# Loading a 2048-element scale vector with one DMA and one broadcast in place of four DMAs and two broadcasts

## The chip, the cores and the metric

The kernel runs on one core of a Trainium2 chip. The metric is device time in microseconds (us) of one execution. The engines that matter here are ScalarE (ACT), VectorE (DVE), GpSimd (POOL), SyncE (SP, which here only issues DMAs), and the 16 DMA engines of the core, which carry every byte between the chip's main memory and the on-chip memory of 128 partitions. A DMA that SP or ACT issues goes into a queue of its issuer (in the profile, q1 is SP's and q10 is ACT's), and is carried out as packets on the DMA engines. TensorE is not used.

## The reference

```python
def setup_inputs():
    B, S, D = 8, 512, 2048
    return {"x": randn(B, S, D) as float32, "gamma": randn(D) as float32}

def reference(x, gamma):
    x_rep = np.repeat(x, 2, axis=1)
    rms = np.sqrt((x_rep ** 2).mean(axis=-1, keepdims=True) + 1e-6)
    return (x_rep / rms * gamma[None, None, :]).astype(np.float32)
```

Each of the 4096 rows of x is divided by its root mean square, multiplied by gamma, and written twice. The input is 33.6 MB, the output 67.1 MB, and gamma 8 KB.

## The kernel before, in words

The 4096 rows are cut into four blocks of 1024 rows. A block is loaded by one DMA of 8.4 MB (`load`, line 50) in which each partition gets 8 whole rows, 65,536 contiguous bytes. Its output, 16.8 MB, leaves by two DMAs of 8.4 MB (`store`, line 53), each again 65,536 contiguous bytes per partition. So there are 4 loads and 8 stores, twelve large DMAs of the same size, all on SP's queue and in the order in which `four` issues them.

There is one large buffer `y` with three regions of 8 rows per partition: `first`, `second` and `third`. `four(n, m, ...)` handles two blocks. It loads block n across the end of `first` and the start of `second`, calls `constants`, loads block m into `third`, and then works through four half blocks. For each half block ACT squares and sums four rows (`squares`, lines 63 and 67), DVE takes the reciprocal (line 76) and multiplies each row by it and by gamma (line 77, `scalar_tensor_tensor`, from the region that holds the input to the region that holds the output), and the result row is copied next to itself by ACT or DVE (`repeat`, line 84). Then SP issues the store. The kernel calls `four` twice, for blocks 0 and 1 and for blocks 3 and 2. The second pair of loads has to wait until the stores that still read their regions have landed.

The order on every engine is as written (`manual_schedule`, line 86); no scheduler moves anything. The first load is issued by SP, then `constants` (lines 122 to 141) puts its work on DVE, ACT and POOL, and then SP issues the second load.

`constants` brings gamma to all 128 partitions. Its DMAs are issued by ACT. One brings the first 2000 elements as 16 pieces of 125 elements (500 bytes), laid down in partition 0 with a step of 256 elements, in a part of `y` that no load touches so early (line 127). Three more bring the last 48 elements, 16 each (64 bytes; line 133). POOL then copies partition 0 to all partitions into `gamma_b`: the 2000 elements (line 137) when the first DMA has landed, and the last 48 (line 141) when the other three have landed. The first multiply on DVE waits for both. It overwrites the place where the pieces of gamma lay, so it also has to come behind POOL's reading of them.

Of the kernel before, what the change touches and what calls it, by code (L numbers as in the profile page):

```python
# [1 line left out]

# [4 lines left out]


@with_exitstack
def kernel(  # L10
    ctx: ExitStack,
    tc: tile.TileContext,
    x: bass.AP,
    gamma: bass.AP,
    out: bass.AP,
):
    nc = tc.nc
    P = nc.NUM_PARTITIONS
    f32 = mybir.dt.float32
    Act = mybir.ActivationFunctionType  # L20
    Alu = mybir.AluOpType

    B, S, D = x.shape
    Bo, So, Do = out.shape
    R = So // S
    assert R == 2 and D == Do and B == Bo and So == S * R
    eps = 1e-6
    inv_d = 1.0 / float(D)


    K = 4
    N = B * S
    ntiles = N // (P * K)
    assert N % (P * K) == 0 and ntiles == 8
    H = 2
    x_t = x.rearrange("b s d -> (b s) d").rearrange("(n p k) d -> n p k d", p=P, k=H * K)
    out_t = out.rearrange("b s d -> (b s) d").rearrange("(n p h j) d -> n h p (j d)", p=P, h=H, j=K * R)

    singles = ctx.enter_context(tc.tile_pool(name="singles", bufs=1))
    rows = ctx.enter_context(tc.tile_pool(name="rows", bufs=1))  # L40
    junk = ctx.enter_context(tc.tile_pool(name="junk", bufs=1, space=bass.MemoryType.PSUM))
    small = ctx.enter_context(tc.tile_pool(name="small", bufs=4))

    y = rows.tile([P, 3 * K * R, D], f32, name="y")
    first, second, third = 0, K * R, 2 * K * R

    def load(n, at):
        nc.sync.dma_start(out=y[:, at : at + H * K, :], in_=x_t[n])  # L50

    def store(n, h, to):
        nc.sync.dma_start(
            out=out_t[n, h], in_=y[:, to : to + K * R, :].rearrange("p j d -> p (j d)")
        )

    def squares(at, rows):

        n = len(rows)
        ss = small.tile([P, n], f32, name=f"ss{n}")  # L60
        for c, k in enumerate(rows):
            sq = junk.tile([P, D], f32, name="sq")
            nc.scalar.activation(  # L63
                out=sq[:], in_=y[:, at + k, :], func=Act.Square, accum_out=ss[:, c : c + 1]
            )
        rms = small.tile([P, n], f32, name=f"rms{n}")
        nc.scalar.activation(out=rms[:], in_=ss[:], func=Act.Sqrt, scale=inv_d, bias=eps_t[:])  # L67
        return rms

    def scale(at, to, rows, rms, at_once=K):  # L70
        n = len(rows)
        rstd = small.tile([P, n], f32, name=f"rstd{n}")
        for c, k in enumerate(rows):
            if c % at_once == 0:
                part = slice(c, min(c + at_once, n))
                nc.vector.reciprocal(out=rstd[:, part], in_=rms[:, part])  # L76
            nc.vector.scalar_tensor_tensor(  # L77
                out=y[:, to + R * k, :], in0=y[:, at + k, :], scalar=rstd[:, c : c + 1],
                in1=gamma_b[:], op0=Alu.mult, op1=Alu.mult,
            )  # L80

    def repeat(to, k0, k1, copy):
        y_r = y[:, to + R * k0 : to + R * k1, :].rearrange("p (k r) d -> p k r d", r=R)
        copy(out=y_r[:, :, 1, :], in_=y_r[:, :, 0, :])  # L84

    ctx.enter_context(tc.manual_schedule())

    half = K // 2
    up, down = list(range(K)), list(range(K - 1, -1, -1))

    def four(n, m, constants, at_once):


        load(n, first + K)
        constants()
        load(m, third)
        for rows, n_at_once in ((up[:half], half), (up[half:], at_once)):
            scale(first + K, first, rows, squares(first + K, rows), n_at_once)
        repeat(first, 0, half, nc.scalar.copy)
        repeat(first, half, K, nc.vector.tensor_copy)  # L100
        store(n, 0, first)
        scale(second, second, down, squares(second, down))
        repeat(second, half, K, nc.scalar.copy)
        repeat(second, 0, half, nc.vector.tensor_copy)
        store(n, 1, second)
        roots = [squares(third + h * K, up) for h in range(H)]
        scale(third, first, up, roots[0])
        repeat(first, 0, half, nc.scalar.copy)
        repeat(first, half, K, nc.scalar.copy)
        store(m, 0, first)  # L110
        scale(third + K, third, up, roots[1])
        repeat(third, 0, K, nc.scalar.copy)
        store(m, 1, third)

    gamma_b = singles.tile([P, D], f32, name="gamma_b")
    G, E = 16, 3
    C = D // G - E
    gamma_s = y[0:1, 0:2, :].rearrange("p k (c d) -> p (k c) d", c=G // 2)
    gamma_t = y[0:1, 2, :]
    eps_t = singles.tile([P, 1], f32, name="eps_t")  # L120

    def constants():
        nc.vector.memset(eps_t, eps)  # L123

        root = singles.tile([P, 1], f32, name="root")[:]
        nc.scalar.activation(out=root, in_=eps_t[:], func=Act.Sqrt)  # L126
        nc.scalar.dma_start(
            out=gamma_s[0:1, :, :C],
            in_=gamma[: G * C].rearrange("(p c d) -> p c d", p=1, c=G),
        )  # L130
        for c in range(E):
            at = G * C + c * G
            nc.scalar.dma_start(
                out=gamma_t[0:1, c * G : (c + 1) * G],
                in_=gamma[at : at + G].partition_broadcast(1),
            )
        nc.gpsimd.partition_broadcast(  # L137
            out_ap=gamma_b[:, : G * C].rearrange("p (c d) -> p c d", c=G),
            in_ap=gamma_s[0:1, :, :C],
        )  # L140
        nc.gpsimd.partition_broadcast(out_ap=gamma_b[:, G * C :], in_ap=gamma_t[0:1, : E * G])  # L141

    four(0, 1, constants, 1)
    four(3, 2, lambda: None, half)


# [1 line left out]
_INS = ['x', 'gamma']  # L148
_OUTS = [((8, 1024, 2048), 'float32')]


# [23 lines left out]
```

## Time and profile before

| what | value |
|---|---|
| median of 3 runs | 238.1 us (238.01 to 238.22) |
| the profiled execution | 237.99 us, its span 236.2 us |
| DMA traffic | 100.68 MB, mean 426 GB/s over the span |
| ACT busy | 110.2 us (47%) |
| DVE busy | 84.5 us (36%) |
| POOL busy | 2.8 us (1%) |
| first load issued | 0.72 us |
| first square on ACT starts | 22.68 us |
| first multiply on DVE starts | 27.34 us |
| first store issued | 39.27 us |

The span is what the profile shows of the execution, from its first to its last instruction; 1.8 us of the execution's time lie around it. A row of the profile that names a line and an engine, such as "L77 DVE", stands for all instructions of that source line on that engine, with their number, the total of their busy time, the mean of one, and the idle time of the engine ahead of them with what ended it. The trace also records every DMA packet with its queue, start, duration and size, and the prediction makes use of these records.

### The profile page before, as it was taken

The numbers are of one execution on the slowest core, as the hardware profiler recorded it, in microseconds if no ns is written. First come the engines' busy times: TensorE is split into PE (matmuls) and PEld (weight loads), VectorE is DVE, ScalarE is ACT, GpSimd is POOL, SyncE is SP. The second block draws the span as 40 slices with busy tenths as digits, with TensorE's granted clock in tenths as the row PEclk, the third lists the DMA queues.
The fourth block names the chain that finished last, engine by engine and source line by source line (L and its number), as shares of the span: only waits on it lengthen the run. The fifth ranks groups of instructions, "written<-read, shape, count | busy, mean of one in ns | idle before, by whom it ended". The sixth has DMA issues, their size and how long they took to land.

```text
span 236.2 us, 226 instructions
## 1 busy us (share of the span) xinstructions
DVE 84.5 (36%) x48; ACT 110.2 (47%) x86; POOL 2.8 (1%) x6
## 2 busy tenths in 40 slices
DVE  0000396594699500000000007928919992000000
ACT  2001989479998470000000049991999957400000
POOL 0210000000000000000000000000000000000000
DMA  9898989989898989989898998989898998989894
GB/s 355 357 533 355 533 355 477 411 377 511 355 533 357 522 366 466 422 377 511 355 533 355 488 400 377 511 355 533 355 533 355 477 411 377 511 355 533 355 533 178
DMA packets 1767, 100.68 MB, mean 426 GB/s; under 512 B 230, under 2 KB 230, under 8 KB 230
## 3 DMA queue, kind: packets, MB, share of 16 engines
q1 hardware_dynamic: 1728, 100.66, 98.8%
q10 hardware_dynamic: 38, 0.01, 0.0%
q14 instruction: 1, 0.01, 0.0%
HBM read 33.56 MB, written 67.11 MB: 426 GB/s over the span
## 4 chain that ended last, share of the span: by engine, by line
DMA 45%; ACT 26%; DVE 12%; issue 2%; DVEq 0%
DMA y<-in_x_dram 26%; DMA out_dram<-y 20%; ACT sq L63 15%; DVE y L77 12%; ACT y L84 11%; ACT rms L67 1%; DVE rstd L76 0%; DVEq L77 0%
## 5 line engine op out<-in xcount | busy, mean ns | idle before, releaser
L63 ACT ACTIVATE sq<-y 128x2048 f32<-128x2048 f32 x32 | 60.1, 1878 | 73.0 <-DMA y<-in_x_dram 72.3
L77 DVE SCALAR_TENSOR_TENSOR y<-y,rstd,gamma_b 128x2048 f32<-128x2048 f32 x32 | 73.8, 2349 | 1.5 <-DMA out_dram<-y 0.9
L84 ACT COPY y<-y 128x4096 f32<-128x4096 f32 (+1 forms) x10 | 42.6, 4283 | 18.9 <-DVE y L77 18.2
L76 DVE RECIPROCAL rstd<-rms 128x4 f32<-128x4 f32 (+2 forms) x11 | 1.9, 168 | 109.2 <-ACT rms L67 109.2
L84 DVE COPY y<-y 128x4096 f32<-128x4096 f32 x4 | 9.2, 2294 | 0.1
L63 ACT ACTIVATION_READ_ACCUMULATOR sq<-y 128x1 f32 x32 | 6.0, 186 | 0.0
L67 ACT ACTIVATE rms<-ss,eps_t 128x4 f32<-128x4 f32 (+1 forms) x10 | 3.0, 296 | 0.3
L137 POOL PARTITION_BROADCAST gamma_b<-y x1 | 2.2, 2243 | 10.2 <-DMA y<-in_gamma_dram 10.2
L126 ACT ACT_TABLE_LOAD x1 | 1.3, 1283 | 0.7 <-PEq L159 0.7
L141 POOL PARTITION_BROADCAST gamma_b<-y x1 | 0.3, 323 | 10.2 <-DMA y<-in_gamma_dram 10.2
L123 DVE MEMSET eps_t<- 128x1 f32 x1 | 0.1, 59 | 0.8 <-PEq L159 0.8
L126 ACT ACTIVATE root<-eps_t 128x1 f32<-128x1 f32 x1 | 0.2, 202 | 0.0
L159 POOL MEMSET const-bfloat16-1.0<- 128x1 bf16 x1 | 0.1, 101 | 0.0
L159 POOL MEMSET const-uint8-127<- 128x1 uint8 x1 | 0.1, 101 | 0.0
L159 POOL MEMSET const-float32-0.0<- 128x1 f32 x1 | 0.1, 98 | 0.2 <-issue 0.2
L159 POOL MEMSET const-float32-1.0<- 128x1 f32 x1 | 0.1, 98 | 0.0
## 6 DMA issues: line engine op xcount, KB each, us to landing
out_dram<-y SPq DMA_DIRECT2D x8, 24.9
y<-in_x_dram SPq DMA_DIRECT2D x4, 31.4
y<-in_gamma_dram ACTq DMA_DIRECT2D x3, 0.1 KB
y<-in_gamma_dram ACTq DMA_DIRECT2D x1, 7.8 KB, 9.6
```

The costliest lines, as they stand in the source:

```text
L63: nc.scalar.activation(out=sq[:], in_=y[:, at + k, :], func=Act.Square, accum_out=ss[:, c : c + 1])
L67: nc.scalar.activation(out=rms[:], in_=ss[:], func=Act.Sqrt, scale=inv_d, bias=eps_t[:])
L76: nc.vector.reciprocal(out=rstd[:, part], in_=rms[:, part])
L77: nc.vector.scalar_tensor_tensor(out=y[:, to + R * k, :], in0=y[:, at + k, :], scalar=rstd[:, c : c + 1], in1=gamma_b[:], op0=Alu.mult, op ...
L84: copy(out=y_r[:, :, 1, :], in_=y_r[:, :, 0, :])
L123: nc.vector.memset(eps_t, eps)
L126: nc.scalar.activation(out=root, in_=eps_t[:], func=Act.Sqrt)
L137: nc.gpsimd.partition_broadcast(out_ap=gamma_b[:, : G * C].rearrange("p (c d) -> p c d", c=G), in_ap=gamma_s[0:1, :, :C],)
L141: nc.gpsimd.partition_broadcast(out_ap=gamma_b[:, G * C :], in_ap=gamma_t[0:1, : E * G])
L159: nc = _bacc.Bacc("TRN2", target_bir_lowering=False, num_devices=1)
```

## The change

The four DMAs of `constants` become one, and the two broadcasts become one. The staging place for gamma is now one row of partition 0 (2048 elements, contiguous), written as 16 pieces of 128 elements that lie one behind the other on both sides. Nothing else is touched: the loads, the stores, the arithmetic and their order stay.

```diff
     gamma_b = singles.tile([P, D], f32, name="gamma_b")
-    G, E = 16, 3
-    C = D // G - E
-    gamma_s = y[0:1, 0:2, :].rearrange("p k (c d) -> p (k c) d", c=G // 2)
-    gamma_t = y[0:1, 2, :]
+    G = 16
+    gamma_s = y[0:1, 0, :].rearrange("p (c d) -> p c d", c=G)
     eps_t = singles.tile([P, 1], f32, name="eps_t")
...
         nc.scalar.dma_start(
-            out=gamma_s[0:1, :, :C],
-            in_=gamma[: G * C].rearrange("(p c d) -> p c d", p=1, c=G),
+            out=gamma_s, in_=gamma.rearrange("(p c d) -> p c d", p=1, c=G)
         )
-        for c in range(E):
-            at = G * C + c * G
-            nc.scalar.dma_start(
-                out=gamma_t[0:1, c * G : (c + 1) * G],
-                in_=gamma[at : at + G].partition_broadcast(1),
-            )
         nc.gpsimd.partition_broadcast(
-            out_ap=gamma_b[:, : G * C].rearrange("p (c d) -> p c d", c=G),
-            in_ap=gamma_s[0:1, :, :C],
+            out_ap=gamma_b[:].rearrange("p (c d) -> p c d", c=G), in_ap=gamma_s
         )
-        nc.gpsimd.partition_broadcast(out_ap=gamma_b[:, G * C :], in_ap=gamma_t[0:1, : E * G])
```

## The prediction

> **What bounds the kernel now.** I read the page's busy shares first. No compute engine is above 47%, so none of them is the bound by itself. The DMA rows say what is: 100.66 MB of the 100.68 MB are on SP's queue, and the DMA engines are busy for 98.8% of the span.
>
> ```profile
> span 236.2 us, 226 instructions
> DVE 84.5 (36%) x48; ACT 110.2 (47%) x86; POOL 2.8 (1%) x6
> DMA packets 1767, 100.68 MB, mean 426 GB/s; under 512 B 230, under 2 KB 230, under 8 KB 230
> q1 hardware_dynamic: 1728, 100.66, 98.8%
> q10 hardware_dynamic: 38, 0.01, 0.0%
> ```
>
> The view of stretches shows where the missing 1.2% lies: in the first 39 us and behind 234 us, not in the middle (last two columns: DMA share, GB/s; a packet counts where it starts, hence 1.01).
>
> ```profile
> 2.00:41.00 39.00, 11.93 (x8) 17.60 (x17) 2.57 (x2) 1.00 0.94 407
> 41.00:118.00 77.00, 30.33 (x16) 36.94 (x27) 0.00 (x0) 1.00 1.01 435
> 118.00:157.00 39.00, 11.85 (x7) 17.43 (x16) 0.00 (x0) 1.00 0.99 430
> 157.00:234.00 77.00, 30.34 (x16) 36.90 (x27) 0.00 (x0) 1.00 1.01 436
> ```
>
> The packet records make it exact. The twelve large DMAs are 1536 packets of 65,536 B, 96 on each of 16 engines. One takes 2.418 us, the next starts 0.004 us before its end, so 96 take 96 x 2.414 = 231.7 us. The first packets start at 1.73 to 2.06 us and take 2.86 to 3.27 us (0.45 to 0.85 more than later ones), engines lose up to 0.67 us more where reading starts again at 118 us, and the last packets end between 234.5 and 235.0 us. Following each engine from packet to packet I find no other idle time on any engine. The time is thus: start, 96 packets on the last engine, and 1.2 us behind them.
>
> The page's chain of waits has ACT and DVE on it, but this chain follows one path of releases. What counts is whether a store is ever issued too late. The DMA issues and the landings in the packet records give two tight places: the first stores of the two passes are issued at 39.27 and 155.20 us, and the first engine runs out of loads at 40.93 and 157.21. The later stores of each pass have 3.4 us or more.
>
> Gamma's own path, from the view of instructions in order:
>
> ```profile
> 0.72 0.86 SPq L50 DMA_DIRECT2D y<-in_x_dram  x2
> 0.89 0.60 ACTq L127 DMA_DIRECT2D y<-in_gamma_dram  x1
> 1.53 0.67 ACTq L133 DMA_DIRECT2D y<-in_gamma_dram  x1
> 2.23 0.50 ACTq L133 DMA_DIRECT2D y<-in_gamma_dram  x2
> 10.62 2.24 POOL L137 PARTITION_BROADCAST gamma_b<-y  x1 [10.19 <-DMA y<-in_gamma_dram]
> 22.68 1.88 ACT L63 ACTIVATE sq<-y 128x2048 f32<-128x2048 f32 x1 [20.47 <-DMA y<-in_x_dram]
> 23.02 0.32 POOL L141 PARTITION_BROADCAST gamma_b<-y  x1 [10.16 <-DMA y<-in_gamma_dram]
> 27.07 0.17 DVE L76 RECIPROCAL rstd<-rms 128x2 f32<-128x2 f32 x1 [26.23 <-ACT rms L67]
> 27.34 4.61 DVE L77 SCALAR_TENSOR_TENSOR y<-y,rstd,gamma_b 128x2048 f32<-128x2048 f32 x2
> 39.27 16.96 SPq L53 DMA_DIRECT2D out_dram<-y  x2
> ```
>
> The reader is to see that gamma_b is ready at 23.34 us, that DVE starts its first multiply at 27.34, and that it was waiting for ACT's square root, not for POOL. Gamma is 4.0 us early.
>
> **The change part by part.**
>
> *ACT's issues.* Four issues (0.60, 0.67, 0.21 and 0.26 us) become one. ACT has nothing to do before 22.68 us, when the first load has landed, so this is worth 0. The cover is 20 us.
>
> *Broadcasts.* 2.24 + 0.32 us become one of 2048 elements; by the larger row 2.24 x 2048/2000 = 2.30 us, by both 2.57. It starts when the new DMA lands. The earliest old landing let POOL start at 10.62 us, the latest at 23.02, so gamma_b is ready between 12.9 and 25.6 us. Both are before 27.07, when DVE has its root: 0. If the new DMA landed with the slowest old row, 1.5 us of cover would still be left.
>
> *Waits.* DVE's second multiply, ACT's first copy and SP's first store each lose their wait for the three small DMAs. These landed by 23 us and the waiters ran later (29.6, 32.03, 39.27): 0.
>
> *DMA packets.* Here is the only thing that touches the bound. In the records the old main DMA is 16 packets of 500 B, one per engine, 26 ns each. Around it the next large packet starts 20 ns behind the end of the former instead of 4 ns before: 24 ns per engine, and 6 ns more for the packet that signals the end. The three small DMAs are not spread out. Each is one packet of 64 B, all on one engine (call it A), and each costs A another 6 to 8 ns twice; on A the large packet behind the 500 B also takes 93 ns longer. A falls 0.14 us behind the other engines; with the common 0.03 it pays 0.17 us.
>
> What the new DMA is, I take from the built program: since its 16 pieces lie one behind the other on both sides, it stands there as one run of 1x2048, of the same form as the three 1x16; the old main DMA stands as 1x16x125. The 1x16 form moved as one packet on one engine, so I expect one packet of 8,192 B on A and nothing on the other 15. The Trainium skill, DMA: Bandwidth & Descriptors, Why a DMA increments its semaphore by 16 and not by 1, says that the engines are chosen by the slowest dimension that is not 1, and that software can split a contiguous 2048-element load so that 16 engines share it. This trace has the unsplit case (64 B on one engine) and no split one. The Trainium skill, same title, Rules for kernel authors, speaks against the change: an outermost dimension under 16 confines a DMA to as many engines. By it the sum is the one that follows; split, it would be that of the first rival.
>
> The nearest row for 8,192 B is one packet that fetches instructions amid the stores:
>
> ```profile
> q14 instruction: 1, 0.01, 4.8%
> ```
>
> It was recorded with 0.309 us at 75.06 us, and the engine that carried it (call it B) fell 0.246 us behind. So A pays 0.25 to 0.31 us plus 0.006 for the signal, in place of 0.17: +0.08 to +0.15 us on A. The other 15 engines save 0.03 each.
>
> *The sum at the end.* B ends last (0.50 us behind the first), A 0.13 us before B. After: B 0.03 earlier, A 0.05 before B to 0.05 behind it. The end moves by -0.03 to +0.02 us if B stays where it is. Whether the instruction fetch still falls on B at 75 us is open, as ACT has fewer instructions; without it B ends 0.25 us earlier and the next engine, 0.13 us before, sets the end; behind 118 us it would be as much later. That is -0.13 to +0.15 us.
>
> *The first store.* The first load lands when its slowest engine signals, at 22.116 us, and this is A. With A 0.08 to 0.15 us later, ACT's squares, the multiplies, the copies and the store's issue all move by as much: 39.35 to 39.43 us. From issue to first packet the first load took 1.00 us, and 1.34 to the last engine. So the store's packets are there at 40.3 to 40.8 us, and engines get free from 40.90: covered, with 0.1 to 0.6 us left. The same holds at 155 us with more room.
>
> Sum against the profiled execution (237.99 us, 0.1 below the median): -0.13 to +0.15 us, most likely within 0.05. I predict the median unchanged, 238.1 us; the three runs shown differ by 0.21 us already. A measurement of this kernel tells little under 0.2%, 0.48 us, from no change.
>
> **The rivals.**
>
> *Spread: the DMA does become 16 packets of 512 B, one per engine.* Then A saves 0.14 us and the other engines pay what they do now. For it: the code asks for 16 pieces. (This is what the Trainium skill, DMA: Bandwidth & Descriptors, says software can do.) Against: the 1x16 row. The end is still engine B's: 238.1 us, no change. So it decides nothing about the time.
>
> *Late store, slower.* The place is the end of the second load, 40.9 us. It decides if a store needs more than 1.5 us from issue to packets. No engine had a gap there, so the need is at most 1.65 us now. If it is just that, the 0.08 to 0.15 us of A's lag becomes a gap on all engines, and an engine that ran dry may pay the start excess of 0.45 to 0.85 again: 238.1 + 0.5 to 1.0 = 238.6 to 239.1 us. Against it: the 1.00 to 1.34 us of the first load.
>
> *Ahead of the first load, slower.* The old main DMA took 0.60 us to issue and its packets came behind two large ones, at 7.1 us. A simpler form may be issued faster (the small ones took 0.21 and 0.26) and its packet may come before A's first large one, at 1.7 us. Then A's own start waits for it: 0.30 us of transfer plus a start of 0.45 to 0.85, less the 0.17 saved, puts A 0.6 to 1.0 us back. A has 0.13 us before it sets the end, so 238.6 to 239.0. Against it: a read that is queued early overlaps the start of the next. For such a start the Trainium skill, DMA: Bandwidth & Descriptors, Latency and other measured facts, gives some 0.8 us as the least round trip to main memory; by that figure this rival is 238.9, and the excess of the trace's first packets agrees.
>
> *Faster.* The start excess shrinks because ACT and SP issue less at the same time (SP's second issue took 0.43 us, later ones 0.34): all engines 0.6 us earlier, 237.5 us. Against it: the excess is on the first load, issued at 0.72 us, before gamma's.
>
> **How the numbers follow.** Forecast (one packet on A, end unmoved, with or without the moved fetch) 0.59; spread 0.17; late store 0.09; ahead of the first load 0.11; faster 0.04. No change is the first two, 0.76; slower 0.20; faster 0.04. The no-change cases reach from 238.1 - 0.13 to + 0.15, widened by the runs' own 0.1 to either side, so 237.8 to 238.4; to hold part of the slower cases the range goes on to their middle, 238.8.
>
> **What would show it.** One packet of 8,192 B on ACT's queue (or 16 of 512 B if it is spread) and no others but its signals; one broadcast of about 2.3 us that ends before 25.6; the first store issued 0.1 us later; DMA share still 1.01 from 41 us on; span 236.1 to 236.4. It is wrong if an engine shows a gap at 41 or 157 us, if the first large packet of one engine starts near 2.4 us or takes over 3.5, or if the broadcast takes several times longer than its 2.3 us and DVE's first multiply has POOL as its releaser.

## The result, and the profile after

The changed kernel takes 238.9 us (median of 7 runs, 238.79 to 239.05) against 238.2 us before (238.01 to 238.31). The ratio is 1.0031 with a 95% interval of 1.0019 to 1.0043: slower by 0.7 us, or 0.3%. The prediction was no change, 238.1 us, with a range to 238.8.

The page of the changed kernel, in the lines that were shown of the kernel before:

```profile
span 236.8 us, 217 instructions
DVE 84.5 (36%) x48; ACT 110.2 (47%) x86; POOL 2.5 (1%) x5
DMA packets 1731, 100.68 MB, mean 425 GB/s; under 512 B 193, under 2 KB 193, under 8 KB 193
q1 hardware_dynamic: 1728, 100.66, 98.5%
q10 hardware_dynamic: 2, 0.01, 0.0%
```

ACT's queue carries two packets: one of 8,192 B and one that signals its end. So the 16 pieces did become one packet on one engine. The stretches (last two columns: DMA share, GB/s) are as full as before, so no engine was starved:

```profile
2.00:41.00 39.00, 11.92 (x8) 17.78 (x17) 2.29 (x1) 1.00 0.95 412
41.00:118.00 77.00, 30.33 (x16) 36.77 (x27) 0.00 (x0) 1.00 1.01 436
118.00:157.00 39.00, 11.85 (x7) 16.99 (x16) 0.00 (x0) 1.00 0.99 430
157.00:234.00 77.00, 30.34 (x16) 37.34 (x27) 0.00 (x0) 1.00 1.01 436
```

Gamma's path, in the view of instructions in order:

```profile
0.89 0.50 ACTq L125 DMA_DIRECT2D y<-in_gamma_dram  x1
8.07 2.29 POOL L128 PARTITION_BROADCAST gamma_b<-y  x1 [7.64 <-DMA y<-in_gamma_dram]
22.55 1.88 ACT L63 ACTIVATE sq<-y 128x2048 f32<-128x2048 f32 x1 [20.33 <-DMA y<-in_x_dram]
27.21 4.61 DVE L77 SCALAR_TENSOR_TENSOR y<-y,rstd,gamma_b 128x2048 f32<-128x2048 f32 x2
39.14 0.35 SPq L53 DMA_DIRECT2D out_dram<-y  x1
```

gamma_b is ready at 10.4 us, 17 us early, and the first store is issued at 39.14 us, 0.13 us earlier than before. Up to here the change cost nothing.

The difference lies at the end. SP's closing waits, on the line that ends the program (columns: number, shortest, median and longest in ns, first and last start in us). The kernel before, from 235 us on:

```profile
L170 SPq EVENT_SEMAPHORE  x1: 28/28/28, 235.3 to 235.3; - x1
L170 SPq DRAIN  x1: 7/7/7, 235.4 to 235.4; - x1
```

The changed kernel, from 235.4 us on:

```profile
L159 SPq EVENT_SEMAPHORE  x4: 27/28/28, 235.8 to 236.0; - x4
L159 SPq DRAIN  x1: 7/7/7, 236.0 to 236.0; - x1
```

Before, the wait for the last store is SP's last wait. After, three more waits stand behind it, although what they wait for landed long ago. They start 62, 64 and 62 ns apart.

Three intervals of the profiled executions, set beside each other (us; the last signal is the last packet on SP's queue):

| | last signal | from there to the span's end | time outside the span | sum |
|---|---|---|---|---|
| before | 234.98 | 1.18 | 1.83 | 237.99 |
| after | 235.42 | 1.36 | 2.19 | 238.96 |
| difference | +0.44 | +0.18 | +0.36 | +0.97 |

The time outside the span hardly scatters: 2.15 to 2.25 us in all seven runs of the changed kernel, 1.78 to 1.89 in those runs of the kernel before that give their span. So 0.18 + 0.36 = 0.54 us are not in the DMA traffic at all. What is left of the medians' 0.7 us is some 0.2 us in the DMA packets. The packet records show one more thing there. Queue q14 (its kind in the profile is "instruction") fetches instructions, 8,192 B in one packet on one engine. This packet was at 75.06 us before. In the changed kernel the DMA view for 152.4 to 152.9 us has it:

```profile
q14 instruction: 1, 0.01, 3.9%
```

So I had three theories: LAG (the 8,192 B on one engine make it end last), TAIL (the closing waits) and AROUND (the time outside the span), and for the remainder the place of this fetch.

The packet records let one follow each engine from packet to packet. Large packets follow one another every 2.414 us, so a delay shows as a break in this rhythm. The fetch costs its engine more than its own 0.309 us, because the large packet behind it is slow too (2.53 to 2.56 us in place of 2.418 with ACT's fetch at 75 us, 2.71 to 2.73 with the fetch at 152 us). The engine falls back by 0.42 to 0.45 us at 75 and by 0.60 us at 152. Gamma's packet of the same size cost its engine 0.31 us; the large packet behind it took 2.418 us.

In the profiled execution of the changed kernel the fetch's engine ends at 235.22 us. Another engine ends last, at 235.42. It lost 0.58 us in one packet at 118.9 us, where the engines turn from stores to loads. Three engines come to that turn within 0.02 us of each other, gamma's among them, and the records do not tell which of them went on to lose the 0.58 us. So this trace alone does not rule LAG out.

### The profile page after: what moved, and what is told of

The parts are those of the page before. It is cut to its first block, busy times and chain, and to the rows that moved or that the text cites. A ratio compares the mean times of both kernels' runs of the same rounds, so it can differ in the third digit from the quotient of the medians.

```text
span 236.8 us, 217 instructions
## 1 busy us (share of the span) xinstructions
DVE 84.5 (36%) x48; ACT 110.2 (47%) x86; POOL 2.5 (1%) x5
## 4 chain that ended last, share of the span: by engine, by line
DMA 45%; ACT 26%; DVE 13%; issue 1%; DVEq 0%; SPq 0%
DMA y<-in_x_dram 26%; DMA out_dram<-y 20%; ACT sq L63 15%; DVE y L77 13%; ACT y L84 11%; ACT rms L67 1%; DVE rstd L76 0%; DVEq L77 0%; SPq L50 0%
```

## The experiments

All diffs are against the changed kernel unless said otherwise, and show only its main lines. The spans below are medians over the runs of each kernel, and the kernel before was run on the same chip each time (median 238.12 to 238.23 us, span 236.3 to 236.4).

**Gamma spread over 16 engines.**

```diff
-    gamma_s = y[0:1, 0, :].rearrange("p (c d) -> p c d", c=G)
+    gamma_s = y[0:1, 0:2, :].rearrange("p k (c d) -> p (k c) d", c=G // 2)[:, :, : D // G]
```

> As the changed kernel, but gamma's 16 pieces of 512 B are laid down with a step of 256 elements, so that they stay apart: still 13 DMAs and one broadcast. Three theories of the 0.7 us. LAG (the one packet of 8,192 B holds one DMA engine back, and this engine ends last): the pieces go to 16 engines, the last large packet ends by 235.0 us again in place of 235.4, and if LAG is all of it the time is 238.2. TAIL (with 13 DMAs in place of 16 SP's closing wait for the last store is followed by three more waits, 0.19 us) and AROUND (the time outside the span is 2.16 in place of 1.83 us, as the instruction streams have other lengths): both stay, so 238.2 + 0.19 + 0.33 = 238.7.

Measured: 238.94 us, ratio 1.0031 (1.0020 to 1.0043), the same as the changed kernel. The DMA view from 1.7 to 12 us shows 32 packets on ACT's queue:

```profile
q10 hardware_dynamic: 32, 0.01, 0.3%
```

These are the 16 pieces and their 16 signals. Spreading them won nothing, so LAG is no part of the 0.7 us. The pattern at the end is that of the changed kernel: the fetch's engine (152.54 us) ends second, at 235.26 us, and another that lost time at the turns ends at 235.53.

**The three small DMAs back, unused.**

```diff
             out=gamma_s, in_=gamma.rearrange("(p c d) -> p c d", p=1, c=G)
         )
+        for c in range(3):
+            nc.scalar.dma_start(
+                out=gamma_t[0:1, c * G : (c + 1) * G],
+                in_=gamma[2000 + c * G : 2016 + c * G].partition_broadcast(1),
+            )
```

(`gamma_t` is `y[0:1, 2, :]`, as before the change.)

> As the changed kernel, with the three small DMAs of 64 B put back beside it (nothing reads them; the one broadcast stays): 16 DMAs again, one packet of 8,192 B. LAG: one engine still is 0.3 us and the small packets' 0.1 us behind and ends last, 235.4 to 235.5 us; if LAG is all, 238.9 to 239.0. TAIL: no wait stands behind the one for the last store, so 0.19 us go: 238.7. AROUND: the time outside the span goes back to about 1.83 us, 0.33 less. TAIL and AROUND together: 238.4.

Measured: 238.13 us, ratio 0.9998 (0.9988 to 1.0008). With 8,192 B on one engine and three packets more to carry, the kernel is as fast as before. The time around the span is 1.83 us, 1.18 us lie behind the last signal, and the fetch stands at 74.94 us. More was won (0.77 us) than TAIL and AROUND together (0.54), so a third part goes with the DMAs, and the place of the fetch is the candidate. The profiled execution was the slowest of this kernel (238.56 us). Its fetch engine ends at 235.03 us, but two others, which lost time at 155 us, end at 235.32 and 235.57. So an early fetch does not make the end early in every execution.

**ACT's stream filled up.** Five idle instructions on ACT bring its stream from 103 instructions back to 108, as before the change.

```diff
         nc.scalar.activation(out=root, in_=eps_t[:], func=Act.Sqrt)
+        pad = singles.tile([P, 5], f32, name="pad")
+        for c in range(5):
+            nc.scalar.activation(out=pad[:, c : c + 1], in_=eps_t[:], func=Act.Sqrt)
```

> As the changed kernel, with five more one-element square roots on ACT in its idle first 20 us, which fill the five instructions that the change took from ACT's stream. AROUND, if ACT's stream is what counts: the time outside the span is 1.83 us again, 238.6, and the instruction fetch is back near 75 us in place of 152. LAG and TAIL: nothing changes, 238.9.

Measured: 238.64 us, 0.3 less than the changed kernel. But the time around the span stayed at 2.20 us: the gain is in the span, 236.4 in place of 236.7 us. The fetch is back, at 75.04 us. The DMA view from 74.9 to 75.4 us:

```profile
q14 instruction: 1, 0.01, 3.9%
```

So this filler undid the part in the DMA packets, and not AROUND, as the theory that named ACT's stream had it. The 238.6 us expected by that theory came out by luck: a different 0.3 us went.

The fillers stand ahead of ACT's DMA issue and so also delay gamma's packet, from 4.9 to 7.4 us. That is not where the gain comes from: with gamma spread (the run above, and the last one below) the pieces come from 7.2 and from 7.1 us on, without and with fillers, and the span still falls from 236.75 to 236.4 us. (The last run also has DVE's filler, which leaves the span at 236.7 us by itself.)

**24 KB more on the same engine.**

```diff
+        nc.scalar.dma_start(
+            out=y[0:1, 1:4, :], in_=x[0:1, 0:3, :]
+        )
```

> As the changed kernel, with one more DMA of 24 KB (three rows of x, which nothing reads) into partition 0, behind gamma's: one more packet on the same engine, 14 DMAs. LAG: 24,576 B at 27.1 B per ns are 0.9 us more on that engine, the last packet ends at 236.2 to 236.4 us and the time is 239.7 to 239.8. If an engine's lag is made up on the way (at 118 us), or the 0.7 us lie elsewhere, 238.8 to 239.0; TAIL has two waits behind the last store's in place of three, 0.06 less.

Measured: 240.15 us, 1.25 us more than the changed kernel and more than the 0.8 to 0.9 expected. So a large enough lag of one engine does move the end and is not made up. Ahead of 118 us its engine was 1.1 us behind the next one. The first load landed 0.74 us later than in the changed kernel (its last signal at 22.91 in place of 22.17) and the first store was issued at 39.89 us. At the turn from loads to stores that follows, at 41 us, the other engines fell back by up to 0.3 us. This is the gap of the rival *late store*, which the 8,192 B did not reach. All engines end late here, the first at 235.32 and the last two together at 236.64 us.

**One instruction on SP, and one on DVE.** The first kernel has a drain on SP between the first two loads; the second a memset on DVE.

```diff
         nc.vector.memset(eps_t, eps)
+        nc.sync.drain()
```

```diff
         nc.vector.memset(eps_t, eps)
+        nc.vector.memset(singles.tile([P, 1], f32, name="pad"), eps)
```

> As the changed kernel, with one idle instruction (a drain) on SP between the first two loads, so that SP's stream has 37 instructions again as in the kernel before (36 in the changed one). AROUND has been 1.83 us with 16 DMAs and 2.2 us with 13 or 14, whatever ACT's stream had. If it is the length of SP's stream that sets it, it is 1.83 us here and the time 238.55; if the length of DVE's stream (66 and 65 instructions), the number of DMAs or the waits behind the last store, it stays 2.2 and the time 238.9.

> As the changed kernel, with one more one-element memset on DVE at the start, so that DVE's stream has 66 instructions again as in the kernel before (65 in the changed one). If DVE's stream sets AROUND: 1.83 us and 238.55. If SP's stream, the number of DMAs or the waits at the end do: 2.2 us and 238.9.

Measured: 238.85 us with SP's instruction, and 2.23 us around the span: no effect. 238.52 us with DVE's, and 1.84 us around the span in the median of 11 runs (1.80 to 1.87); its span of 236.7 us is that of the changed kernel. One instruction of 59 ns, at a time when DVE had nothing to do, takes 0.36 us off the execution. DVE had lost one instruction in the change: in the built program a separate wait ahead of the second multiply, for the three small DMAs.

**15 DMAs.** Two of the three small DMAs are put back.

> As the changed kernel, with two of the three small DMAs put back (nothing reads them): 15 DMAs, SP 37 and DVE 66 instructions, ACT 106. TAIL: one wait behind the one for the last store, 0.06 us more than with 16 DMAs, so from the last signal to the span's end 1.24 us (1.18 with 16, 1.31 with 14, 1.36 with 13). AROUND by the streams of SP or DVE: 1.83 us, and the time 238.2 to 238.5 by where ACT's fetch falls; AROUND by the number of DMAs or by any wait behind the last: 2.2 us, 0.37 more.

Measured: 238.32 us, ratio 1.0008 (0.9999 to 1.0016), 1.82 us around the span. From the last signal to the span's end it takes 1.25 us, as TAIL has it. Over the kernels this interval is 1.18 us with 16 DMAs, 1.25 with 15, 1.31 with 14 and 1.36 with 13: none, one, two and three waits behind the last store's. The fetch stood at 152.5 us here, and its engine ends at 235.22 us. Against the kernel with all three small DMAs (238.13 us, fetch at 74.94) this one is 0.19 us slower. One closing wait makes 0.07 of that, so only 0.12 us are left here for the late fetch.

**16 fillers on ACT in place of 5.**

> As the changed kernel, with 16 more one-element square roots on ACT in its idle first 20 us in place of the 5 tried before. If it counts that ACT's instruction fetch falls before 118 us, where the DMA engines turn from stores to loads and are brought together again, any earlier place does: the fetch before 75 us, 238.64 as with 5. If the 5 helped by ACT's stream ending at the same place as before, 238.9.

Measured: 238.50 us, span 236.3. The gain of the five is there again, but the fetch stands at 75.08 us and no earlier. So this run did not try a third place for the fetch, as was meant. It shows that the five do not help by ending ACT's stream where it ended before, since 16 do the same.

**Both fillers.** Five on ACT, one on DVE.

> The changed kernel with both fillers: five one-element square roots on ACT and one one-element memset on DVE, both at the start, where the engines are idle. One packet of 8,192 B and 13 DMAs as in the changed kernel. If the parts add up (0.36 us around the span by DVE's stream, some 0.3 us by the place of ACT's instruction fetch, 0.18 us by the three waits behind the last store, nothing by the 8,192 B on one engine), only the waits are left: 238.2 to 238.3, 0.1 to 0.2 above the kernel before, span 236.3 to 236.4 and 1.83 us around it. If ACT's or DVE's filler worked in another way, they overlap: 238.5.

Measured: 238.16 us, ratio 0.9998 (0.9990 to 1.0007), span 236.3, around it 1.82. The first line of its page, and the first line of the page with DVE's filler alone:

```profile
span 236.3 us, 223 instructions
```

```profile
span 236.7 us, 218 instructions
```

The parts add up: 238.9 - 0.36 - 0.3 = 238.2. Gamma still comes in one packet on one engine, by one broadcast. So nothing that the change does to gamma costs time that can be seen; what it took from the instruction streams does. The 0.18 us of closing waits are still in this kernel (1.37 us behind the last signal), yet it equals the kernel before in the median. The runs of the kernel before scatter upwards more, with spans of 236.2 to 237.0 us.

**An extra DMA of 8 KB early and late, from memory to memory.** On top of both fillers, a row of x into a scratch row, issued by ACT ahead of the second `repeat` of the third half block, in the first or the second pass.

> As the kernel with both fillers, with one more DMA of 8,192 B (a row of x into a scratch row of the main memory, which nothing reads) on ACT's queue at about 76 us, amid the stores of the first pass: 14 DMAs, two waits behind the last store. One packet of 8,192 B on one engine ahead of 118 us, where the engines are brought together again: no cost, 238.2, 0.06 below the kernel with both fillers. If such a packet costs what it takes wherever it falls, 238.5.

> The same extra DMA of 8,192 B at about 192 us, amid the stores of the second pass. Behind 118 us nothing brings the engines together before the end, so if the fetch at 152 us cost its 0.3 us by falling behind that point, this packet's engine ends 0.25 to 0.3 us later, and the time is 238.2 to 238.5 by how near the last that engine is. If the place does not matter, it equals the kernel with the early one.

Measured: 238.15 and 238.18 us. The two runs say nothing on the question, for in the packet records this DMA is 16 packets of 512 B, one per engine. They say that 16 small packets, early or late, cost nothing that can be seen.

**Eight instructions on DVE.** The memset above eight times.

> The changed kernel with eight more one-element memsets on DVE at the start, 73 instructions in its stream (65 in the changed kernel, 66 before). If the time around the span falls once DVE's stream is over 65 long, it is 1.83 us and the time 238.5, as with one memset. If it goes by the stream's length modulo some block, it may be 2.2 us (238.9) or a third value; under 1.83 it would point to a kernel faster than both.

Measured: 238.66 us, with 1.76 us around the span and the span at 236.9. The DMA view from 150 to 200 us has two fetches:

```profile
q14 instruction: 2, 0.02, 0.1%
```

They are at 152.5 and 191.3 us, and none comes behind the span's end any more. With 65 or 66 instructions on DVE there was a fetch behind the end. The first line is from the DMA view of the changed kernel from 238.4 to 238.9 us, the second from that of the kernel before from 237.3 to 237.8 us:

```profile
q14 instruction: 1, 0.01, 4.8%
```

```profile
q14 instruction: 1, 0.01, 5.7%
```

It comes 1.69 to 1.95 us behind the span's end in the kernels with 65 instructions (1.71 in the changed one) and 1.18 to 1.48 us behind it in those with 66 (1.19 in the kernel before). As it went into the span when DVE's stream grew, it is DVE's. It comes later where the execution outside the span is longer. Within each group the two do not go together, though (1.95 us behind the end with 16 fillers on ACT, and still 2.19 us outside), so it is not shown that this fetch is what the time outside waits for.

Inside the span, at 191 us, the fetch costs its engine 0.69 us, and this engine ends last, at 235.43 us. The span is 0.2 us longer than the changed kernel's; some 0.1 us of this lies behind the last signal (1.46 in place of 1.36 us).

**One packet on one engine, early and late.** As the two runs from memory to memory, but into a spare tile in partition 0, 7,040 B in one run.

```diff
+        if extra:
+            nc.scalar.dma_start(out=spare[:], in_=x[0:1, 0, :1760])
         repeat(first, half, K, nc.scalar.copy)
```

> The kernel with both fillers, with one more DMA of 7,040 B into a spare tile in partition 0 (nothing reads it), one run and so one packet on one engine, on ACT's queue at about 75 us, ahead of the turn from stores to loads at 118 us. 14 DMAs. If a lag that arises ahead of 118 us is made up there: 238.1 to 238.2, as the kernel with both fillers.

> The same DMA of 7,040 B at about 191 us, behind the last point at which the engines are brought together. If a packet on one engine costs by its place, as the fetch at 152 us seems to (span 236.7 against 236.4), this engine ends up to 0.25 us later: 238.2 to 238.4, and above the early one by up to 0.25. If place does not matter, and ACT's filler worked in another way, the two are equal.

Measured: late 238.47 us, 0.3 us more than with both fillers alone and a little over the 238.2 to 238.4 expected. The engine of the packet, which comes at 189.1 us, is the last one at the end. Against the kernel before on the same chip the ratio is 1.0006 (0.9994 to 1.0018), so this difference is not clear of the noise. Early 239.18 us, the opposite of what was expected. The DMA view from 75.1 to 75.5 us shows the one packet:

```profile
q10 hardware_dynamic: 1, 0.01, 4.2%
```

In the packet records its engine loses 0.36 and 0.34 us at the turn at 118 us and 0.54 us more at the turn at 155 us, and ends last by 0.5 us. So the turns do not help a late engine: they hold back early ones, and can hold back a late one further. The kernel before shows the first at 118 us: the engine of the fetch loses nothing in the packet ahead of the turn (2.418 us), others up to 0.67 us. It comes to the turn 0.25 us behind the next engine and leaves it 0.04 us behind.

**40 instructions on DVE** (with ACT's five).

> The kernel with both fillers, with 40 one-element memsets on DVE in place of one. With 73 instructions on DVE a second instruction fetch stood at 191 us inside the span, the time around the span was 1.76 us, and the last packet was late (235.4 us). If it is DVE's fetch that sets the time around the span and its place that sets what it costs inside, the fetch now falls ahead of 118 us: 1.76 us around, span 236.3 to 236.4, 238.1. If its place does not matter: span 236.5 or more.

Measured: 238.45 us. DVE's fetch is at 67.8 us, ACT's at 74.9, and 1.80 us lie around the span (1.76 expected). But the span is 236.7, not 236.3 to 236.4. In the packet records the engine of DVE's fetch falls back by 0.66 us and becomes the latest, 0.22 us behind where the latest was; it is the last at the end too, at 235.12 us. One fetch before 118 us cost nothing that could be seen, two have a span that is 0.3 to 0.4 us longer. The time itself is not clear of the noise (ratio to the kernel before 1.0004, 0.9991 to 1.0016).

**The early packet with gamma spread, and both fillers with gamma spread.**

> The kernel with both fillers and the one extra packet of 7,040 B at 75 us, but with gamma in 16 pieces on 16 engines. With gamma in one packet of 8,192 B this extra packet cost 1.0 us, at 191 us only 0.3. If it cost so much because the two packets fell on the same engine, which then came last to the turns at 118 and 155 us and lost more there, then without gamma's 0.3 us on it the early packet is free: 238.2 us. If an early packet on one engine costs by itself, as the place alone: 239.1.

> The kernel with both fillers, gamma in 16 pieces on 16 engines. The spread alone made no difference beside the changed kernel, whose end was set by the fetch at 152 us. If it makes none either where that fetch is at 75 us, 238.15 as with the one packet; if the one engine's lag shows once the fetch no longer covers it, 0.1 to 0.2 us less.

Measured: 239.16 us (238.33 to 239.97) for the first. The early packet costs its 1.0 us without gamma's on the same engine, so the sum of two packets on one engine falls as its reason. Why a lone packet at 75 us costs 1.0 us, with so wide a scatter, stays open: ACT's fetch at the same time puts its engine 0.42 to 0.45 us back, the lone packet only 0.27, and the fetch cost nothing that can be seen. 238.23 us for the second: beside the fetch at 75 us, too, it makes no difference whether gamma is in one packet or in 16.

**What makes up the 0.7 us:**

| part | size | shown by |
|---|---|---|
| outside the span, by the length of DVE's stream | 0.36 us | one memset on DVE takes it away, as does the wait that two or three small DMAs bring back (1.82 and 1.83 us); an instruction on SP or ACT does not |
| instruction fetch of ACT at 152 in place of 75 us | about 0.3 us; 0.12 between the kernels with 15 and 16 DMAs | fillers on ACT take it away (spans 236.3 and 236.4 against 236.7); the fetch moves with them, and its engine ends at 235.2 to 235.3 in place of 234.9 to 235.1 us |
| three closing waits on SP | 0.18 us | 1.18, 1.25, 1.31 and 1.36 us from the last signal to the span's end with 16, 15, 14 and 13 DMAs |
| gamma in one packet on one engine | 0 | spreading it changes nothing, beside either place of the fetch |

The parts sum to about 0.8 us, a little over the 0.7 measured. The second is the least certain in size. What the place of the fetch does to its engine is in the records. In the six profiled executions with ACT's fetch at 152 us (the changed kernel, gamma spread, one instruction on SP, one on DVE, eight on DVE, 15 DMAs) its engine is one of the three earliest ahead of the fetch, falls back by 0.60 us, and ends second, at 235.22 to 235.29 us. (In the changed kernel, and in the one with both fillers, two engines start a packet together right behind the fetch; I took the one whose packet is slow, as in the others.) In the twelve with the fetch at 75 us, the kernel before among them, it ends at 234.92 to 235.13 us, 0.24 us earlier in the mean. With the 1.36 us behind it, 235.22 gives a span of 236.6 us, the shortest that the changed kernel shows (236.6 to 236.9). What comes on top in single executions is another engine that loses time at the turns. Why the large packet behind a fetch is slower at 152 than at 75 us is open, and that an early packet is harmless as such is not shown.

## Why the prediction was wrong

*What bounds the kernel: right.* All 96 packets per engine go through without a gap, before and after. The time is made of the start, 96 packets on the last engine and what lies behind them, and a change that touches none of the compute stages still moved it.

*ACT's issues and broadcasts: right. Waits: right in what they released.* There is one issue of 0.50 us and one broadcast of 2.29 us (2.30 predicted). It is done at 10.4 us, ahead of the 12.9 to 25.6 us given, as gamma's packet came at 4.9 us. DVE still waits for ACT's square root.

*DMA packets: right in form and in price.* One packet of 8,192 B and 0.309 us on one engine was read from the form 1x2048 in the built program. It cost its engine 0.31 us, the upper end of 0.25 to 0.31. The place of A was misread: followed through the turn at 118 us, A ends 0.33 us ahead of B, not 0.13, so there was more room for it than the sum gives. The Trainium skill, DMA: Bandwidth & Descriptors, Why a DMA increments its semaphore by 16 and not by 1, on the choice of engines by the slowest dimension that is not 1, agrees with both forms that ran: 1x2048, which the instruction carries as one element of 8,192 B, was one packet, and 16x128 was 16. The Trainium skill, same title, Rules for kernel authors, which spoke against the change, is borne out in the mechanism: the DMA was confined to one engine. Here this cost no time that can be seen.

*The first store: right in that it stayed covered, wrong in its direction.* It was issued 0.13 us earlier, not 0.08 to 0.15 later. The first load's last signal did come later, by 0.05 us (22.17 against 22.12). But ACT's first square starts 0.38 us behind that signal, and in the kernel before it started 0.56 us behind it. In all other kernels run here it is 0.33 to 0.39 us, also with the three small DMAs put back. Why it was longer in the kernel before is open.

*The sum at the end: wrong.* Three of its terms failed. The first was "1.2 us behind them", taken for a constant with the time around the span. Both depend on the kernel. They grew by 0.18 us (closing waits, as the number of DMAs decides where the last store's wait stands) and by 0.36 us (one instruction less on DVE). I had listed the removed waits and costed each by what it released; a wait also is an instruction in a stream, and its removal shortened DVE's stream by one and ACT's by five with the DMAs. The second was the moved instruction fetch, which I named as open and gave +0.15 us at most; it cost 0.1 to 0.4 us between the pairs of kernels that differ in it. Its price was misread: 0.246 us is how far B stands behind the next engine once the fetch has passed. Against its own rhythm B lost 0.45 us, as the large packet behind the fetch is slow too, and at 152 us it is 0.60 us. "behind 118 us it would be as much later" was too little for another reason as well: it left out what the turn at 118 us does for an early fetch. B came to this turn 0.25 us behind the next engine and left it 0.04 us behind. The third was the range: the two rivals on the slower side were other mechanisms (a late store, gamma's packet ahead of the first load), and neither happened, so 238.8 as its upper end had no cause behind it.

*The rivals.* Spread: did not happen, and as a kernel of its own it made no difference, as was written. Late store: not in the changed kernel; the 24 KB run showed it. Ahead of the first load: the packet came at 4.9 us, behind the first large packet. One sign named for this rival did appear, without the rival: the first large packets of two engines started only at 2.39 and 2.74 us. They took 2.60 and 2.52 us and so ended no later than the others. Faster: no.

## What to carry to other kernels

Where a kernel is at its transfer limit and a change is worth tenths of a microsecond, the instruction streams are part of the change: count the instructions that each engine gains or loses, waits included, and look for the packets that fetch instructions and for the closing waits. Before such a change is called slower, run it once with idle instructions that bring the streams back to their old length, at a time when the engines have nothing to do; here this undid all of a 0.3% loss.

Look in the packet records at what a small DMA has become. Here runs that lie contiguous on both sides, from main memory into one partition, were one packet on one DMA engine (64 to 24,576 B), also where the code writes 16 pieces; a step on one side kept the pieces apart. A contiguous run of 8,192 B from memory to memory was 16 packets of 512 B on 16 engines.

## What was not expected of the hardware

- One memset of 59 ns on DVE at the start shortens the execution by 0.36 us, all of it outside the span. With 65 instructions on DVE the time outside was 2.14 to 2.26 us, with 66 it was 1.77 to 1.90, and with 73 or 105 it was 1.73 to 1.83.
- Fetching instructions takes part in the DMA traffic: 8,192 B in 0.309 us on one engine, which falls back by more than that, 0.42 to 0.45 us (ACT's fetch at 75 us), 0.60 us (ACT's at 152) or 0.66 to 0.69 us (DVE's at 68 and 191). The Trainium skill, Runtime: NRT & Kernel Launch, Instruction fetch mechanics, gives blocks of 16 KiB and calls the cost of crossing into one mostly hidden. The packets here are of 8 KB, and one at 152 us in place of 75 cost about 0.3 us.
- This fetch jumps: with 103 to 106 instructions on ACT it was at 152 to 154 us, with 107 to 119 at 75 us.
- Closing waits on SP that have long been met take 62 to 64 ns each.
- A lone packet of 7,040 B on one engine cost 1.0 us at 75 us, which is not explained, and 0.3 us at 189 us, which is not clear of the noise.
